# Three norms between layers: rows scaled by r on VectorE and transposed in pairs of k tiles between the first products

## The chip, the core and the metric

The kernel runs on one core of a Trainium2 chip. The metric is the device time of one execution in microseconds (us). The median of three runs of the kernel before is 2278.21 us (2277.64 to 2278.24). The engines are PE (TensorE, products and transposes), DVE (VectorE), ACT (ScalarE), POOL (GpSimd) and SP (which issues the DMAs).

## The reference, cut to what matters

Two layers work on 256 latent rows of 2048 columns. Each layer has two norms; the first norm of the first layer belongs to the start and isn't touched. The other three are all of this form (`g`, `scale` and `shift` are vectors over the 2048 columns), and each is followed by a product with a large weight:

```python
def rms_norm(x, g):
    xf = x.astype(jnp.float32)
    y = xf * lax.rsqrt(jnp.mean(xf * xf, axis=-1, keepdims=True) + EPS)
    return (y * g.astype(jnp.float32)).astype(x.dtype)

def modulate(h, shift, scale):
    return h * (1.0 + scale[:, None, :]) + shift[:, None, :]
...
    x = x + gt1[:, None, :] * yl
    x = x + gt2[:, None, :] * sq_relu_mlp(modulate(rms_norm(x, g_norm_ffn[layer]), sh2, sc2),
                                          w_ffn_up[layer], w_ffn_down[layer])
```

## The kernel before, in words

The rows lie in two blocks of 128 (`x0`, `x1`, in rows of `order` below `x_5691` and `x_5692`), the 2048 columns in 16 k tiles of 128. For a product the activations must stand transposed, as eight tiles `xt_92` to `xt_99` with a pair of k tiles each; every tile holds a rounded part and the rest of it (`split`: the rounding is an ACT CAST, L388, the rest a DVE subtraction, L389). Weights arrive in `raw` buffers of 128 x 2048 (1 MB) and are split in the same way into parts of 128 x 1024, `hi` on ACT (L184) and `lo` on DVE (L185), with three buffers for each. A part holds four k tiles of `group_b` (L255, the FFN's first product: 4 products for a k tile, two of 512 and two of 256 columns) or two of `group_a` (6 products of 512 columns for a k tile).

A norm starts in `residual`: after the last 256 columns of x are there, ACT sums their squares, DVE forms `ms`, POOL raises it to -1/2 (`rr`, L290), once for each block of rows. DVE then writes a diagonal matrix with r on it (`diag`, L434). `norm_modulate` (L349) multiplies each 128 x 128 piece of x with it, which transposes and scales in one product (`ps_t`, 32 products, which PE runs as 64 passes); then ACT or DVE applies scale and shift (`mtmp`, L381 and L379; `acol` is the column of factors, L352), and `split` writes the pair.

The three places are called norm 1 (before the first FFN, at 684 us), norm 2 (before the pool layer, at 1416 us) and norm 3 (before the second FFN, at 1545 us).

A scheduler puts the instructions of each engine into one fixed order when the program is built, by priorities: the splitting of weights has the highest (`SOONER`), the norm comes next (`FIRST`), and the background work, 320 steps `acc` on DVE (L311) that form the modulation vectors of later stages from `araw` buffers (NA4 = 7 of them), a low one (`LATER`). `hold` is a list of instructions behind which the next weight parts are put, `norm` the one behind which the background steps are put. On the chip every engine takes its instructions in that order.

Of the kernel before, what the change touches and what calls it, by code (L numbers as in the profile page):

```python
# [36 lines left out]
NA4 = 7  # L37
# [113 lines left out]
class Builder:  # L151
    def __init__(self, nc, tc, I, out):
        self.nc, self.tc, self.I, self.out = nc, tc, I, out
        self.bg = deque()
# [4 lines left out]
        self.hold, self.norm = [], None
        self.hp = None  # L160
        self.gate_pool = None
        self.nraw2 = 2
# [62 lines left out]
    def group_a(self, chunks, lhs, blocks=(0, 1), cols=512):  # L225
# [9 lines left out]
        for i, ch in enumerate(chunks):  # L235
# [4 lines left out]
            for k, b in pairs:  # L240
# [3 lines left out]
                self.mm(o, xh, h, kt + k == 0, False)  # L244
# [104 lines left out]
    def norm_modulate(self, xs, stat, sh, sc, gi):  # L349
        nc = self.nc  # L350
        a = self.tp.tile([P, KT], F32, tag="acol", bufs=1, name="acol")
        nc.vector.scalar_tensor_tensor(a, sc, 1.0, self.gcol[:, gi, :], ALU.add, ALU.mult)  # L352
# [16 lines left out]
        for kp in range(KT // 2):  # L369
            if kp >= N_PRE:  # L370
                transposed(kp, 0)
            transposed(kp, 1)
            ps = pss[kp]
# [16 lines left out]

    def keep_warm(self, n):

        ps = self.pa.tile([P, 192], F32, tag="ax", name="ps_warm")
        with self.tc.issue_after(self.last_mm):
            for _ in range(n):
                self.mm(ps, self.ident, self.mask, True, True)
# [4 lines left out]
    def residual(self, ps, c, w, gate, stat, after=None):  # L401
# [8 lines left out]
        with self.tc.high_priority(offset=FIRST):  # L410
# [9 lines left out]
            else:  # L420
# [4 lines left out]
                if after is None:  # L425
                    self.diag = self.cp.tile([P, 2, P], F32, tag="diag", bufs=1, name="diag")
                for b in range(2):
# [5 lines left out]
                    if after is None:  # L433
                        self.last_diag = nc.vector.tensor_scalar(self.diag[:, b], self.ident, self.r[b], None, ALU.mult).ins  # L434
# [514 lines left out]
    def pool_layer(self, stat, sh, sc, gate):  # L949
# [177 lines left out]
```

## Time and profile before

| | us |
|---|---|
| median of three runs | 2278.21 |
| the profiled execution, its time | 2277.29 |
| its span | 2275.5 |
| PE busy | 2240.6 (98%) |
| DVE busy | 1686.8 (74%) |
| ACT busy | 1101.2 (48%) |

The span is that of the instructions; 1.8 us of the execution's time lie around it. PE is busy nearly throughout, so time is gained or lost where PE waits or does other work than products. At the three norms PE has no products for some 10 us.

### The profile page before, as it was taken

The numbers are of one execution on the slowest core, as the hardware profiler recorded it, in microseconds if no ns is written. First come the engines' busy times: TensorE is split into PE (matmuls) and PEld (weight loads), VectorE is DVE, ScalarE is ACT, GpSimd is POOL, SyncE is SP. The second block draws the span as 40 slices with busy tenths as digits, with TensorE's granted clock in tenths as the row PEclk, the third lists the DMA queues.
The fourth block names the chain that finished last, engine by engine and source line by source line (L and its number), as shares of the span: only waits on it lengthen the run. The fifth ranks groups of instructions, "written<-read, shape, count | busy, mean of one in ns | idle before, by whom it ended". The sixth has DMA issues, their size and how long they took to land.

```text
span 2275.5 us, 31625 instructions
## 1 busy us (share of the span) xinstructions
PE 2240.6 (98%) x12514; PEld 1864.4 (82%) x12514; DVE 1686.8 (74%) x2053; ACT 1101.2 (48%) x1482; POOL 36.6 (2%) x47
## 2 busy tenths in 40 slices
PE   8999999999999999999999999999999999999998
PEld 4667788778888888888888888888888888888887
DVE  4569999988868877887888875769864655556655
ACT  4226465554446544544544554445444443443443
POOL 0000000001000000000000000000000000000000
PEclk9999999999999999999999999999999999999999
DMA  9876776777886888888888885646865555555553
GB/s 359 294 273 225 269 258 252 259 284 287 319 299 253 320 311 305 297 320 303 324 316 310 298 302 199 222 171 252 309 230 195 185 187 195 182 192 188 185 190 125
DMA packets 110637, 582.72 MB, mean 256 GB/s; under 512 B 12292, under 2 KB 12420, under 8 KB 66584
## 3 DMA queue, kind: packets, MB, share of 16 engines
q1 hardware_dynamic: 110488, 580.70, 70.3%
q8 instruction: 98, 1.61, 0.3%
q14 instruction: 51, 0.42, 0.0%
HBM read 578.55 MB, written 2.10 MB: 255 GB/s over the span
## 4 chain that ended last, share of the span: by engine, by line
PE 88%; DVE 5%; ACT 2%; issue 2%; DMA 2%; POOL 0%; SPq 0%; POOLq 0%; DVEq 0%; ACTq 0%
PE mma L221 39%; PE mmb L221 34%; PE mmf L221 4%; PE mmn L221 3%; PE mmi L221 2%; DVE acc L311 1%; DVE lo L185 1%; PE ps_as L221 1%; PE ps_o L221 1%; ACT hi L184 1%; PE ps_ada L221 1%; DVE kk L731 1%; DVE qg L731 0%; DMA raw<-in_w_fbs 0%; DMA xraw<-in_ctx 0%
## 5 line engine op out<-in xcount | busy, mean ns | idle before, releaser
L184 ACT CAST hi<-raw 128x1024 fp32r<-128x1024 f32 (+1 forms) x701 | 733.1, 1047 | 945.4 <-PE mma L221 455.1
L185 DVE TENSOR_TENSOR lo<-raw,hi 128x1024 fp32r<-128x1024 f32 (+1 forms) x701 | 849.9, 1215 | 417.3 <-ACT hi L184 416.0
L221 PE MATMUL mma<-hi,xt 128*128 128x512 f32 x2800 | 872.8, 391 | 0.5 <-DVE q L280 0.5
L221 PE MATMUL mmb<-xt,hi 128*128 128x512 f32 x2304 | 813.6, 398 | 1.1 <-DVE xt L389 0.8
L221 PE MATMUL mmb<-xt,lo 128*128 128x256 f32 x2304 | 648.1, 281 | 0.8 <-DVE lo L185 0.8
L221 PEld LDWEIGHTS mma<-hi,xt 128*128 128x128 f32 x2800 | 524.7, 188 | 111.6 <-DVE q L280 1.0
L221 PE MATMUL mma<-lo,xt 128*128 128x512 f32 x1400 | 546.4, 390 | 0.0
L221 PEld LDWEIGHTS mmb<-xt,hi 128*128 128x128 f32 x2304 | 432.9, 188 | 104.1 <-DVE xt L389 1.0
L311 DVE SCALAR_TENSOR_TENSOR acc<-araw,csil,acc 128x1024 f32<-128x1024 f32 x320 | 409.5, 1280 | 49.9 <-DMA araw<-in_wada 48.2
L221 PEld LDWEIGHTS mmb<-xt,lo 128*128 128x128 f32 x2304 | 436.2, 189 | 3.1 <-DVE lo L185 1.1
L221 PEld LDWEIGHTS mma<-lo,xt 128*128 128x128 f32 x1400 | 263.0, 188 | 55.3 <-issue 0.2
L221 PE MATMUL mmf<-xt,hi 128*128 128x512 f32 x512 | 165.1, 395 | 0.0
L221 PEld LDWEIGHTS mmf<-xt,hi 128*128 128x128 f32 x512 | 96.0, 188 | 26.6 <-ACT hi L184 4.2
L221 PE MATMUL mmf<-xt,lo 128*128 128x512 f32 x256 | 100.2, 391 | 0.0
L221 PE MATMUL mmn<-hi,xt 128*128 128x256 f32 x416 | 76.0, 283 | 0.0
L221 PEld LDWEIGHTS mmn<-hi,xt 128*128 128x128 f32 x416 | 65.3, 192 | 0.4
L221 PE MATMUL mmn<-lo,xt 128*128 128x256 f32 x208 | 58.9, 283 | 0.0
L221 PEld LDWEIGHTS mmf<-xt,lo 128*128 128x128 f32 x256 | 48.1, 188 | 9.5
L221 PE MATMUL mmi<-hi,xt 128*128 128x512 f32 x128 | 45.0, 410 | 6.2 <-ACT xt L550 4.0
L713 ACT COPY both<-kk 128x256 f32<-128x256 f32 x64 | 26.3, 411 | 50.4 <-DVE kk L731 41.6
L389 DVE TENSOR_TENSOR xt<-hup,xt 128x512 fp32r<-128x512 f32 x64 | 43.9, 687 | 8.7 <-ACT xt L388 8.5
L586 DVE TENSOR_TENSOR fbacc<-mmf,fbacc 128x1024 f32<-128x1024 f32 x24 | 29.3, 1221 | 22.1 <-PE mmf L221 22.1
(185 smaller groups left out, 1340.0 us busy)
## 6 DMA issues: line engine op xcount, KB each, us to landing
araw<-in_wada SPq DMA_DIRECT2D x320, 512.0 KB
raw<-in_w_up SPq DMA_DIRECT2D x128, 1024.0 KB
raw<-in_w_down SPq DMA_DIRECT2D x128, 1024.0 KB
sraw<-in_wada_s SPq DMA_DIRECT2D x56, 512.0 KB
raw<-in_w_out SPq DMA_DIRECT2D x16, 1024.0 KB
raw<-in_w_pool SPq DMA_DIRECT2D x16, 1024.0 KB
raw<-in_w_fb SPq DMA_DIRECT2D x10, 1024.0 KB
raw<-in_w_q SPq DMA_DIRECT2D x8, 1024.0 KB
```

The lines of the kernel that those rows point to most:

```text
L184: nc.scalar.copy(hi, raw[:, o:o + w])
L185: nc.vector.tensor_sub(lo, raw[:, o:o + w], hi.bitcast(F32))
L221: self.first_mm = self.nc.tensor.matmul(out, lhsT, rhs, start=start, stop=stop, **kw).ins
L311: nc.vector.scalar_tensor_tensor(acc, raw, self.csil[:, c, 0:1], acc, ALU.mult, ALU.add)
L389: return self.nc.vector.tensor_sub(x[:, :, lo], src, x[:, :, hi].bitcast(F32))
L586: nc.vector.tensor_add(fbacc[h], ps, fbacc[h])
L713: nc.scalar.copy(o.rearrange("p (s j i) -> p j s i", j=2, i=hh), bass.AP(src.tensor, src.offset, [list(src.ap[0]), [st + hh, 2], [seg, ns] ...
L731: nc.vector.tensor_mul(x, x, m.broadcast_to([P, ns, hh]))
```

## The change

Rows of x are scaled by r on DVE (`xn`, 128 x 256, for one pair of k tiles and one block of rows) and transposed by PE's transpose, instead of being multiplied with a diagonal matrix. `diag` goes. Three pairs are prepared at once, as before (N_PRE). The other five stand in `later` and are put out one by one between the products of the first group, ahead of each even k tile (`next_pair`). The first pair has its scale and shift, its rounding and its rest done for each k tile apart. `hold` now lets the first two weight parts go where they will and puts the third behind the first pair, the fourth behind the third pair; background steps are put behind the third pair. `hi` and `lo` get four buffers each, the background's staging six instead of seven. In the pool layer the first product is written ahead of the work on `srow` and `brow`.

```diff
-NA4 = 7
+NA4 = 6
-HELD = 1
+NW = 4
...
-            hi = self.wp.tile([P, 1024], F32R, tag="hi", bufs=3, name="hi")[:, 0:w]
-            lo = self.wp.tile([P, 1024], F32R, tag="lo", bufs=3, name="lo")[:, 0:w]
+            hi = self.wp.tile([P, 1024], F32R, tag="hi", bufs=NW, name="hi")[:, 0:w]
+            lo = self.wp.tile([P, 1024], F32R, tag="lo", bufs=NW, name="lo")[:, 0:w]
             with ExitStack() as st:
-                if self.hold:
-                    st.enter_context(self.tc.issue_after(self.hold.pop(0)))
+                behind = self.hold.popleft() if self.hold else None
+                if behind:
+                    st.enter_context(self.tc.issue_after(behind()))
...
-                        self.mm(ps[:, n], h3[:, j, n * P:n * P + P], xt[kt][:, 0:2, :], kt == 0, False)
-                        self.mm(ps[:, n, 1], l3[:, j, n * P:n * P + P], xt[kt][:, 1, :], False, kt == n_kt - 1)
+                        with self.next_pair(kt if n == 0 else 1):
+                            self.mm(ps[:, n], h3[:, j, n * P:n * P + P], xt[kt][:, 0:2, :], kt == 0, False)
+                        self.last_mm = self.mm(ps[:, n, 1], l3[:, j, n * P:n * P + P], xt[kt][:, 1, :], False, kt == n_kt - 1)
...
-        diag = self.diag
-        self.hold, self.norm = [self.last_diag], self.last_diag
-        pss = {}
+        xn, pss, done = {}, {}, {}
 
         def transposed(kp, b):
-
             if kp not in pss:
-                pss[kp] = self.pa.tile([P, 2, T], F32, tag="ax", name="ps_t")
+                xn[kp] = self.t2("xn")
+                pss[kp] = [self.pa.tile([P, 1, T], F32, tag="ax", name="ps_t") for _ in range(2)] if kp == 0 else \
+                    [self.pa.tile([P, 2, T], F32, tag="ax", name="ps_t")]
+            nc.vector.tensor_scalar(xn[kp][:, b], xs[b][:, 2 * kp * P:2 * kp * P + T], self.r[b], None, ALU.mult)
             for j in range(2):
-                kt = 2 * kp + j
-                self.mm(pss[kp][:, j, b * P:b * P + P], xs[b][:, kt * P:kt * P + P], diag[:, b], True, True)
...
+                o = pss[kp][j][:, 0] if kp == 0 else pss[kp][0][:, j]
+                self.last_mm = nc.tensor.transpose(o[:, b * P:b * P + P], xn[kp][:, b, j * P:j * P + P], self.ident).ins
+
+        def modulated(kp):
             tmp = self.t2("mtmp")
+            x = self.xt2[kp]
...
+                if j if kp == 0 else kp % 2:
+                    nc.vector.tensor_scalar(tmp[:, j], src, s, t, ALU.mult, ALU.add)
                 else:
-                    nc.scalar.activation(tmp[:, j], ps[:, j], AF.Identity, bias=t, scale=s)
-            self.hold.append(self.split(kp, 1, 0, tmp).ins)
-        self.hold = self.hold[:HELD]
+                    nc.scalar.activation(tmp[:, j], src, AF.Identity, bias=t, scale=s)
+                if kp == 0:
+                    nc.scalar.copy(x[:, j, 1], tmp[:, j])
+                    done[kp] = nc.vector.tensor_sub(x[:, j, 0], tmp[:, j], x[:, j, 1].bitcast(F32)).ins
+            if kp:
+                done[kp] = self.split(kp, 1, 0, tmp).ins
+
+        def ahead(kp):
+            with self.tc.high_priority(offset=FIRST):
+                for b in range(2):
+                    transposed(kp, b)
+                modulated(kp)
...
+        for kp in range(N_PRE):
+            transposed(kp, 1)
+            modulated(kp)
+        self.norm = done[N_PRE - 1]
+        self.later = deque(lambda kp=kp: ahead(kp) for kp in range(N_PRE, KT // 2))
+
+        self.hold = deque([None, None, lambda: done[0], lambda: done[2]])
+
+    def next_pair(self, kt):
+
+        if self.later and kt % 2 == 0:
+            with self.tc.issue_after(self.last_mm):
+                self.later.popleft()()
+            return self.tc.issue_after(self.last_mm)
+        return nullcontext()
...
-                    if after is None:
-                        self.last_diag = nc.vector.tensor_scalar(self.diag[:, b], self.ident, self.r[b], None, ALU.mult).ins
...
         self.plan(LEFT_P, 18)
+        pooled(0)
...
-        for n in range(4):
+        for n in range(1, 4):
             pooled(n)
```

How this moves instructions, at the places that the prediction speaks of. PE at norm 1 before: after the last product of the layer (not shown) the filling product `ps_warm`, all 32 products with the diagonal matrix, then the products `mmb` of the first pair:

```order
L221 MATMUL ps_warm<-small,ident 128x192
L221 MATMUL ps_t<-diag,x_5691 128x128 x8
L221 MATMUL ps_t<-diag,x_5692 128x128 x8
L221 MATMUL ps_t<-diag,x_5691 128x128 x2
L221 MATMUL ps_t<-diag,x_5692 128x128 x2
```

PE at norm 1 now, first the start and then the passage from the first pair's eight products to the second pair's:

```order
L222 MATMUL ps_warm<-small,ident 128x192
L370 MATMUL ps_t<-ident,xn 128x128 x16
L222 MATMUL mmb<-xt_92,hi 128x512
L222 MATMUL mmb<-xt_92,lo 128x256
L222 MATMUL mmb<-xt_92,hi 128x512
```
```order
L222 MATMUL mmb<-xt_92,hi 128x512
L222 MATMUL mmb<-xt_92,lo 128x256
L370 MATMUL ps_t<-ident,xn 128x128 x4
L222 MATMUL mmb<-xt_93,hi 128x512
L222 MATMUL mmb<-xt_93,lo 128x256
```

Four pairs are transposed ahead of the first product instead of eight, the others four transposes at a time between the products.

DVE at norm 1 before, from `acol` on:

```order
L352 SCALAR_TENSOR_TENSOR acol<-sc_0_101,small 128x16
L434 TENSOR_SCALAR diag<-ident,rr 128x128
L311 SCALAR_TENSOR_TENSOR acc<-araw,csil,acc 128x1024
L379 TENSOR_SCALAR mtmp<-ps_t,acol,sh_0_100 128x256 x3
L389 TENSOR_TENSOR xt_92<-mtmp,xt_92 128x2x256
L389 TENSOR_TENSOR xt_93<-mtmp,xt_93 128x2x256
L379 TENSOR_SCALAR mtmp<-ps_t,acol,sh_0_100 128x256 x2
L389 TENSOR_TENSOR xt_94<-mtmp,xt_94 128x2x256
L379 TENSOR_SCALAR mtmp<-ps_t,acol,sh_0_100 128x256
L185 TENSOR_TENSOR lo<-raw_6583,hi 128x1024 x2
L185 TENSOR_TENSOR lo<-raw,hi 128x1024
L389 TENSOR_TENSOR xt_95<-mtmp,xt_95 128x2x256
```

DVE at norm 1 now, from `acol` on, in two pieces that follow each other:

```order
L358 SCALAR_TENSOR_TENSOR acol<-sc_0_101,small 128x16
L367 TENSOR_SCALAR xn<-x_5691,rr 128x256 x3
L367 TENSOR_SCALAR xn<-x_5692,rr 128x256 x3
L380 TENSOR_SCALAR mtmp<-ps_t,acol,sh_0_100 128x256 x2
L367 TENSOR_SCALAR xn<-x_5691,rr 128x256
L367 TENSOR_SCALAR xn<-x_5692,rr 128x256
L385 TENSOR_TENSOR xt_92<-mtmp,xt_92 128x256 x2
```
```order
L380 TENSOR_SCALAR mtmp<-ps_t,acol,sh_0_100 128x256 x2
L367 TENSOR_SCALAR xn<-x_5691,rr 128x256
L367 TENSOR_SCALAR xn<-x_5692,rr 128x256
L380 TENSOR_SCALAR mtmp<-ps_t,acol,sh_0_100 128x256
L425 TENSOR_TENSOR xt_94<-mtmp,xt_94 128x2x256
L186 TENSOR_TENSOR lo<-raw_6542,hi 128x1024 x2
L186 TENSOR_TENSOR lo<-raw,hi 128x1024 x2
L425 TENSOR_TENSOR xt_95<-mtmp,xt_95 128x2x256
L367 TENSOR_SCALAR xn<-x_5691,rr 128x256
L425 TENSOR_TENSOR xt_96<-mtmp,xt_96 128x2x256
L367 TENSOR_SCALAR xn<-x_5692,rr 128x256
L425 TENSOR_TENSOR xt_93<-mtmp,xt_93 128x2x256
```

The subtraction that finishes the second pair, `xt_93`, stood second among the pairs and ahead of the weight parts; now it stands fifth, behind four `lo`. Behind it (not shown) come three `acc`, an `mtmp` and the next `lo`.

DVE at norm 3 before, from the second `diag` on, and now, from the first `lo` on (ahead of it stand the same seven rows as at norm 1):

```order
L434 TENSOR_SCALAR diag<-ident,rr 128x128
L185 TENSOR_TENSOR lo<-raw,hi 128x1024 x2
L185 TENSOR_TENSOR lo<-raw_13746,hi 128x1024
L389 TENSOR_TENSOR xt_92<-mtmp,xt_92 128x2x256
L379 TENSOR_SCALAR mtmp<-ps_t,acol,sh_1_104 128x256 x4
L389 TENSOR_TENSOR xt_94<-mtmp,xt_94 128x2x256
L389 TENSOR_TENSOR xt_93<-mtmp,xt_93 128x2x256
```
```order
L186 TENSOR_TENSOR lo<-raw_13805,hi 128x1024
L380 TENSOR_SCALAR mtmp<-ps_t,acol,sh_1_104 128x256 x2
L367 TENSOR_SCALAR xn<-x_5691,rr 128x256
L367 TENSOR_SCALAR xn<-x_5692,rr 128x256
L380 TENSOR_SCALAR mtmp<-ps_t,acol,sh_1_104 128x256
L425 TENSOR_TENSOR xt_95<-mtmp,xt_95 128x2x256
L367 TENSOR_SCALAR xn<-x_5691,rr 128x256
L367 TENSOR_SCALAR xn<-x_5692,rr 128x256
L425 TENSOR_TENSOR xt_94<-mtmp,xt_94 128x2x256
L186 TENSOR_TENSOR lo<-raw_13805,hi 128x1024
L425 TENSOR_TENSOR xt_96<-mtmp,xt_96 128x2x256
L425 TENSOR_TENSOR xt_93<-mtmp,xt_93 128x2x256
```

Three `lo` stood in DVE's row ahead of every pair; now two stand among the pairs, and `xt_93` is again the fifth pair to be finished. At norm 2 the order is like that of norm 3, with three `lo` and four pairs, `xt_93` the fourth of them.

## Rows read from the trace of the kernel before

**Rows 1.** Page, part 1: busy us, share of the span, instructions of each engine.
```profile
PE 2240.6 (98%) x12514; PEld 1864.4 (82%) x12514; DVE 1686.8 (74%) x2053; ACT 1101.2 (48%) x1482; POOL 36.6 (2%) x47
```
**Rows 2.** PE's longest entry of waits, 190 to 540 us: us, times, longest.
```profile
PE ps_sc L221 <- ACT both L713: 4.8, 7, 2.0
```
**Rows 3.** Timeline at norm 1: start us, us, engine, line, operation, count, idle before.
```profile
684.42 0.28 PE L221 MATMUL mmn<-hi,xt 128*128 128x256 f32 x1
...
687.03 0.17 DVE L352 SCALAR_TENSOR_TENSOR acol<-sc,small 128x16 f32<-128x16 f32 x1 [0.67 <-POOL rr L290]
...
687.46 5.87 PE L221 MATMUL ps_t<-diag,x 128*128 128x128 f32 x48 [0.65 <-DVE diag L434]
...
692.53 2.96 ACT L184 CAST hi<-raw 128x1024 fp32r<-128x1024 f32 x3
...
693.62 3.50 DVE L185 TENSOR_TENSOR lo<-raw,hi 128x1024 fp32r<-128x1024 f32 x3
...
694.90 0.39 PE L221 MATMUL mmb<-xt,lo 128*128 128x256 f32 x1 [0.76 <-DVE lo L185]
```
**Rows 4.** Chain in order of time, behind norms 1 and 2: start us, us, what.
```profile
694.90 88.80 PE mmb L221 x511
...
1428.25 22.93 PE mma L221 x101
```
**Rows 5.** Timeline at norm 2.
```profile
1418.76 0.18 DVE L352 SCALAR_TENSOR_TENSOR acol<-sc,small 128x16 f32<-128x16 f32 x1 [0.66 <-POOL rr L290]
...
1428.01 0.71 PE L221 MATMUL mma<-hi,xt 128*128 128x512 f32 x2
```
**Rows 6.** Timeline at norm 3.
```profile
1548.11 0.17 DVE L352 SCALAR_TENSOR_TENSOR acol<-sc,small 128x16 f32<-128x16 f32 x1 [0.66 <-POOL rr L290]
...
1552.40 1.89 DVE L379 TENSOR_SCALAR mtmp<-ps_t,acol,sh 128x256 f32<-128x256 f32 x4
...
1556.16 0.36 PE L221 MATMUL mmb<-xt,lo 128*128 128x256 f32 x1
```
**Rows 7.** DVE's groups by shape: busy us, mean ns of one, idle before.
```profile
L185 DVE TENSOR_TENSOR lo<-raw,hi 128x1024 fp32r<-128x1024 f32 x690 | 842.2, 1222 | 407.3 <-ACT hi L184 406.0
L311 DVE SCALAR_TENSOR_TENSOR acc<-araw,csil,acc 128x1024 f32<-128x1024 f32 x320 | 409.5, 1280 | 49.9 <-DMA araw<-in_wada 48.2
L389 DVE TENSOR_TENSOR xt<-mtmp,xt 128x512 fp32r<-128x512 f32 x24 | 15.8, 686 | 0.5 <-ACT xt L388 0.5
L379 DVE TENSOR_SCALAR mtmp<-ps_t,acol,sh 128x256 f32<-128x256 f32 x24 | 12.0, 537 | 0.1
L414 DVE TENSOR_TENSOR x<-x,rtmp 128x256 f32<-128x256 f32 x16 | 6.7, 422 | 0.3
L484 DVE TENSOR_SCALAR xraw<-xraw,r 128x1024 f32<-128x1024 f32 x4 | 2.9, 749 | 1.3 <-POOL r L290 1.3
L434 DVE TENSOR_SCALAR diag<-ident,rr 128x128 f32<-128x128 f32 x6 | 1.7, 283 | 1.8 <-POOL rr L290 1.8
```
**Rows 8.** Tile `ps_t` (ns min/median/max), then PE's timeline at the start.
```profile
L542 PE MATMUL ps_t<-ident,xraw x64: 272/273/455, 24.0 to 167.4; 128*128 128x128 f32 x64
...
147.01 1.07 PE L542 MATMUL ps_t<-ident,xraw 128*128 128x128 f32 x8
147.84 0.48 PE L221 MATMUL mmf<-xt,hi 128*128 128x512 f32 x1
```
**Rows 9.** Stretches: length, busy us (count) of PE, PEld, DVE, ACT, POOL; PEclk; DMA share, GB/s.
```profile
15.60:19.80 4.20, 1.66 (x18) 0.50 (x16) 1.93 (x7) 1.15 (x1) 1.20 (x2) 0.98 0.99 389
...
20.00:22.00 2.00, 1.69 (x16) 0.59 (x16) 0.39 (x1) 0.69 (x2) 0.00 (x0) 0.50 1.05 420
...
52.00:56.00 4.00, 1.11 (x5) 0.44 (x4) 3.80 (x7) 3.56 (x6) 0.00 (x0) 1.00 1.02 381
```
**Rows 10.** Chain in order of time, at the start.
```profile
26.99 2.93 PE mmi L221 x6
30.92 1.58 PE mmi L221 x6
```

More of the change, by code (lines that the diff above doesn't have):

```diff
@@ L158, in __init__ @@
         self.n_sraw = 0
-        self.hold, self.norm = [], None
+        self.hold, self.later, self.norm = deque(), deque(), None
         self.hp = None
@@ L243, in group_a @@
                 o = outs[blocks.index(b)]
-                self.mm(o, xh, h, kt + k == 0, False)
+                with self.next_pair(kt + k if b == blocks[0] else 1):
+                    self.mm(o, xh, h, kt + k == 0, False)
                 self.mm(o, xh, l, False, False)
@@ L351, in norm_modulate @@
         a = self.tp.tile([P, KT], F32, tag="acol", bufs=1, name="acol")
-        nc.vector.scalar_tensor_tensor(a, sc, 1.0, self.gcol[:, gi, :], ALU.add, ALU.mult)
+        with self.tc.high_priority(offset=SOONER):
+            nc.vector.scalar_tensor_tensor(a, sc, 1.0, self.gcol[:, gi, :], ALU.add, ALU.mult)
         self.keep_warm(N_WARM)
-        diag = self.diag
-        self.hold, self.norm = [self.last_diag], self.last_diag
-        pss = {}
+        xn, pss, done = {}, {}, {}
         def transposed(kp, b):
             if kp not in pss:
-                pss[kp] = self.pa.tile([P, 2, T], F32, tag="ax", name="ps_t")
+                xn[kp] = self.t2("xn")
+                pss[kp] = [self.pa.tile([P, 1, T], F32, tag="ax", name="ps_t") for _ in range(2)] if kp == 0 else \
+                    [self.pa.tile([P, 2, T], F32, tag="ax", name="ps_t")]
+            nc.vector.tensor_scalar(xn[kp][:, b], xs[b][:, 2 * kp * P:2 * kp * P + T], self.r[b], None, ALU.mult)
             for j in range(2):
-                kt = 2 * kp + j
-                self.mm(pss[kp][:, j, b * P:b * P + P], xs[b][:, kt * P:kt * P + P], diag[:, b], True, True)
-        for kp in range(N_PRE):
-            transposed(kp, 0)
[L369 to L373, printed above, removed]
+                o = pss[kp][j][:, 0] if kp == 0 else pss[kp][0][:, j]
+                self.last_mm = nc.tensor.transpose(o[:, b * P:b * P + P], xn[kp][:, b, j * P:j * P + P], self.ident).ins
+        def modulated(kp):
             tmp = self.t2("mtmp")
+            x = self.xt2[kp]
             for j in range(2):
@@ L377, in norm_modulate, with keep_warm @@
                 s, t = a[:, kt:kt + 1], sh[:, kt:kt + 1]
-                if kp % 2:
-                    nc.vector.tensor_scalar(tmp[:, j], ps[:, j], s, t, ALU.mult, ALU.add)
-                else:
-                    nc.scalar.activation(tmp[:, j], ps[:, j], AF.Identity, bias=t, scale=s)
-            self.hold.append(self.split(kp, 1, 0, tmp).ins)
-        self.hold = self.hold[:HELD]
+                src = pss[kp][j][:, 0] if kp == 0 else pss[kp][0][:, j]
+                if j if kp == 0 else kp % 2:
+                    nc.vector.tensor_scalar(tmp[:, j], src, s, t, ALU.mult, ALU.add)
+                else:
+                    nc.scalar.activation(tmp[:, j], src, AF.Identity, bias=t, scale=s)
[10 more added lines that the diff above has]
+        for kp in range(N_PRE):
+            transposed(kp, 0)
+        for kp in range(N_PRE):
+            transposed(kp, 1)
[9 more added lines that the diff above has]
+        return nullcontext()
+    def keep_warm(self, n):
+        ps = self.pa.tile([P, 192], F32, tag="ax", name="ps_warm")
+        with self.tc.issue_after(self.last_mm):
+            for _ in range(n):
+                self.last_mm = self.mm(ps, self.ident, self.mask, True, True)
     def split(self, kp, hi, lo, src):
@@ L389, in split @@
         return self.nc.vector.tensor_sub(x[:, :, lo], src, x[:, :, hi].bitcast(F32))
[L391 to L396, printed above, removed]
     def grow(self, gate, c, w):
@@ L424, in residual @@
                 self.r = [self.cp.tile([P, 1], F32, tag="rr", bufs=4, name="rr") for _ in range(2)]
-                if after is None:
-                    self.diag = self.cp.tile([P, 2, P], F32, tag="diag", bufs=1, name="diag")
                 for b in range(2):
@@ L432, in residual @@
                     self.rstd(ms, self.r[b], 1)
-                    if after is None:
-                        self.last_diag = nc.vector.tensor_scalar(self.diag[:, b], self.ident, self.r[b], None, ALU.mult).ins
         for b in range(2):
```

## The prediction

> **What bounds the kernel now.** The page's first part comes first [rows 1]: PE is busy for 2240.6 us, 98% of the span. So a change counts by what it does to the stretches in which PE has no products, and three of those lie at the norms. The timeline there shows their length. At norm 1 the last product of the layer starts at 684.42, and the stream of products begins at 694.90; between them lie the products with `diag` and the waits [rows 3]. What ends the wait is DVE: `acol` starts at 687.03, once POOL has the second r, and the first `lo` is done 7.87 us after that. At norm 2 the distance from `acol` to the stream is 1428.01 - 1418.76 = 9.25 us with 5 products done before it [rows 5], at norm 3 1556.16 - 1548.11 = 8.05 us, also with 5 done [rows 6]. I count everything from `acol`, since the way to it (last product, residual, squares, POOL) is untouched. In the stream one FFN product takes 88.80 / 511 = 0.174 us, one of the pool layer 22.93 / 101 = 0.227 us [rows 4].
>
> **The change, part by part.** *PE's own work.* 64 passes with `diag` for each norm go and 32 transposes come. Eight transposes stand within 0.83 us (147.01 to 147.84), 0.104 us each [rows 8]; I take 0.107. The passes cost at most 5.87 / 48 = 0.122 us [rows 3]. That is 32 x 0.107 = 3.4 us instead of up to 7.8 for each norm. It would be the gain if PE were what is waited for. It isn't: at all three norms the stream begins when DVE lets it, so this saving counts only where it lies behind that point.
>
> If transposes didn't overlap, each would take its whole duration of 0.273 us [rows 8]; 32 of them would be 8.7 us, and the 12 that stand behind the critical point below would add 12 x (0.273 - 0.107) = 2.0 us at each norm, 6 in all. The Trainium skill ("TensorE: Matmul & The Clock Gate", Part 4: PE-mode transpose) gives about 275 ns for a transpose in a kernel's context and would so lead a reader to that sum. The trace agrees with it as a duration; as a distance it shows 0.104.
>
> *DVE's work.* `diag` goes (0.28 us, twice), 16 `xn` come. The trace has no such shape. The line through 128 columns (283 ns) and 1024 columns (749 ns) gives 350 ns at 256; its bounds are 283 and the 422 of an addition of 256 columns [rows 7]. Back to back, instructions overlap: three `lo` of 1.222 take 3.50, so 1.14 apart [rows 3], four `mtmp` of 0.537 take 1.89, so 0.45 apart [rows 6], an overlap of 0.085. That gives 0.265 for an `xn`, 0.34 for half of a pair's subtraction (422 ns), 0.60 for a whole one (686 ns).
>
> *The order on DVE is the term that decides.* DVE takes its row in order, and the changed row puts the second pair's subtraction, `xt_93`, behind others. PE's row puts the second pair's products straight behind the first pair's eight and four transposes; they wait for `xt_93`. What stands ahead of it from `acol` on, norm 1: `acol` 0.09, 12 `xn` 3.18, 5 `mtmp` 2.25, two halves of `xt_92` 0.68, `xt_94`, `xt_95`, `xt_96` 1.80, four `lo` 4.56, then `xt_93` itself 0.69. Sum 13.25, with PE's wake-up 13.3 us. None of these waits for long on others by my count: ACT's first `hi` can start some 4.6 us after `acol` (before it: one `mtmp`, three casts, two `mtmp`) and then runs 0.95 apart [rows 3], ahead of the `lo`. So pair 2 begins 13.3 us after `acol`, where before the whole stream began at 7.87. By then 8 of 128 products of the first two outputs are done. PE can't use the gap: its row is in order too.
>
> Behind `xt_93` stand three `acc` of 1.28 (each on the sum of the one before, 1.32 apart), an `mtmp` and the next `lo`: 3.96 + 0.45 + 1.22 = 5.6 us, so that `lo` is there at 18.9. PE reaches the product that needs it after 17 products and 4 transposes, 13.3 + 3.4 = 16.7: another wait of 2.1. Norm 1 to the end of the second output: 13.3 + 120 x 0.174 + 12 x 0.107 + 2.1 = 37.6 us; before, 7.87 + 127 x 0.174 = 30.0. **Norm 1: +7.6.**
>
> Norm 3 has two `lo` ahead of `xt_93` instead of four: 13.25 - 2.28 = 10.97, so 11.0; then the same, 11.0 + 20.9 + 1.3 + 2.2 = 35.4. Before: 8.05 + 123 x 0.174 = 29.45. **Norm 3: +5.9.**
>
> Norm 2: 11 `xn` 2.92, 5 `mtmp` 2.25, halves 0.68, two pairs 1.20, three `lo` 3.42, `acol` 0.09, `xt_93` 0.69: 11.25, so 11.3. PE has 14 of the first output's 96 products done by then (the second pair's first two need no subtraction): 11.3 + 82 x 0.227 + 12 x 0.107 = 31.2, and some 0.5 for a pair's `xn` behind a `lo`: 31.7. Before: 9.25 + 91 x 0.227 = 29.9. **Norm 2: +1.8.**
>
> *The clock.* Until now each hole was filled with products with `diag`; now PE has 16 short transposes and eight products in some 15 us. In this trace PE's granted clock fell to 0.50 (1.2 GHz) at 20 us, after a stretch of 4.2 us with 1.66 us of work [15.6 to 19.8, rows 9]; it stayed at 1.00 through 52 to 56 us with 1.11 us of work in 4 [rows 9]. Six products at the low clock took 2.93 us instead of 1.58 [rows 10], and the clock was back behind them: 1.35 us for a fall. I take one fall in the three norms, +1.4; bounds 0 and three falls with their transposes, about +5.
>
> *The buffers.* Fourth `hi` and `lo`: no gain in the stream, where PE waits for no part [rows 4], 511 products without a stop. In the mixer PE's largest wait is for `both`, 4.8 us [rows 2], behind a full DVE; an earlier `lo` may take some of it, a missing staging buffer may add to DVE's 48.2 us of waits for `araw` [rows 7]. I take 0, from -4.8 to +2.4 (two of those 1.2 us waits on the path). *`pooled(0)` moved ahead*: the work on `srow` and `brow` goes behind the first product, where PE has products for 20 us; 0, and if that cover is gone 1 to 2 us once.
>
> **Sum.** 7.6 + 1.8 + 5.9 + 1.4 = 16.7 on the execution's own 2277.29: 2294.0. The median of the runs lies 0.92 above that execution, so 2295 us.
>
> **Rivals.** *DVE keeps up, PE is the bound (not slower).* Place: the second pair at norms 2 and 3. If `xt_93` were there when the first pair's products end, the stream would begin 3.9 us after `acol` (`acol`, eight `xn`, two `mtmp`, the halves: 0.09 + 2.12 + 0.90 + 0.76) with 16 transposes still to pay, 1.7: 5.6 against 8.05 - 5 x 0.17 = 7.2 at norm 3 and 9.25 - 1.1 = 8.1 at norm 2; nothing at norm 1, where the weights themselves are late (first `hi` at 692.53 [rows 3]). Gain 1.6 + 2.5 = 4.1, with the median 2274. It decides from the point where `xt_93` ends under 5.6 us after `acol`; some 5.5 us of work would have to leave DVE's row. With the wait of 4.8 us in the mixer gone too [rows 2] it would be 2269. For it: PE's work does shrink. Against it: the row above.
>
> *The buffers pay part back.* The wait of 4.8 us goes and the clock holds: 2295 - 4.8 - 1.4 = 2289; if part of the wait at norm 1 is filled as well, some 2284.
>
> *The clock falls at every norm and the transposes run at half pace:* 2295 + 2 x 1.4 + 1 to 3 = 2299 to 2301. *The transposes don't overlap:* 2295 + 6 = 2301; the rows speak against it, 0.02. (That is the Trainium skill's 275 ns taken as a distance.)
>
> That the change doesn't do what it says, transposes between products, is no case: the order shows that it does, for four of the eight pairs.
>
> **How the numbers follow.** My forecast (the order on DVE decides, 2290 to 2299) 0.70; clock (0.08) or transposes (0.02) dearer, 2299 to 2302: 0.10; buffers pay back (2284 to 2290) 0.08; the holes half of what I sum and the buffers' gain on top (2278 + 8 - 5 = 2281) 0.06; DVE keeps up 0.06, of which 0.02 at 2274 and 0.04 with the buffers' gain at 2269. A difference under 0.2% (4.6 us) can't be told from none here. Slower by over 0.2%: 0.70 + 0.10 + 0.08 = 0.88; within: 0.06 + 0.02 = 0.08; faster 0.04. The range, 2285 to 2302, leaves out the last two cases and the edge of the third.
>
> **What would show it.** Right: PE's waits of the changed kernel list `mmb` for the DVE subtraction of the second pair at 4 us, twice, and for `lo` at 2 us; the distance from `acol` to the first product on `xt_93` is 13.3, 11.3 and 11.0 us; the stretches between the norms are as long as before. `xn` at 0.35 us and transposes 0.107 us apart show the terms; the granted clock in the holes shows the fall. Wrong: if the second pair's products follow the first pair's without a wait, the order isn't what sets them; if the holes are as summed and the time isn't, the buffers in the mixer moved it.

## The result, and the profile after

The changed kernel takes 2296.6 us (median of 5 runs, 2295.07 to 2299.78) against 2278.24 for the kernel before, measured beside it. The ratio is 1.0079, interval 1.0067 to 1.0091: it is slower by 18 us. The forecast was 2295.

PE's work has hardly changed, and its waits have. Page, part 1, of the changed kernel (engine, busy us, share, instructions), to be held against [rows 1]:

```profile
PE 2240.1 (98%) x12418; PEld 1859.1 (81%) x12418; DVE 1698.0 (74%) x2101; ACT 1102.8 (48%) x1482; POOL 35.7 (2%) x47
```

PE's longest waits in the whole changed kernel (engine, tile and line waited with, what for: us, times, longest); [rows 2] was the longest before:

```profile
PE mmb L222 <- DVE xt L425: 7.6, 2, 4.2
PE ps_t L370 <- DVE xn L367: 6.4, 6, 2.7
...
PE ps_s L222 <- ACT kwt L764: 2.9, 4, 1.3
...
PE mma L222 <- ACT xt L424: 2.1, 1, 2.1
PE ps_sc L222 <- ACT both L738: 2.0, 4, 0.9
...
PE mma L222 <- DVE xt L425: 1.1, 1, 1.1
```

The products now wait for activations. Where that is, the timeline at norm 1 shows (start us, us, engine, line, operation, count, idle before). It answers to [rows 3]:

```profile
688.28 3.89 ACT L185 CAST hi<-raw 128x1024 fp32r<-128x1024 f32 x4
...
690.47 4.63 DVE L186 TENSOR_TENSOR lo<-raw,hi 128x1024 fp32r<-128x1024 f32 x4
691.74 0.29 PEld L222 LDWEIGHTS mmb<-xt,lo 128*128 128x128 f32 x1 [2.08 <-DVE lo L186]
...
692.07 1.14 ACT L424 CAST xt<-mtmp 128x512 fp32r<-128x512 f32 x2
...
695.01 0.69 DVE L425 TENSOR_TENSOR xt<-mtmp,xt 128x512 fp32r<-128x512 f32 x1
...
696.84 0.69 DVE L425 TENSOR_TENSOR xt<-mtmp,xt 128x512 fp32r<-128x512 f32 x1 [0.88 <-ACT xt L424]
697.45 0.35 DVE L367 TENSOR_SCALAR xn<-x,rr 128x256 f32<-128x256 f32 x1
697.71 0.69 DVE L425 TENSOR_TENSOR xt<-mtmp,xt 128x512 fp32r<-128x512 f32 x1
698.31 3.92 DVE L314 SCALAR_TENSOR_TENSOR acc<-araw,csil,acc 128x1024 f32<-128x1024 f32 x3
...
698.55 0.53 PE L222 MATMUL mmb<-xt,hi 128*128 128x512 f32 x1 [3.45 <-DVE xt L425]
```

`acol` starts at 683.59 here. PE has the first pair's products behind it at 694, transposes the next pair, and then waits 3.45 us. DVE is never free in that time but for 0.88 us: it splits four weight parts and finishes three other pairs, and the subtraction at 697.71 is that of the second pair. At norm 3 the same wait is 4.15 us, at norm 2 2.13 and 1.15.

One measure serves for all runs below: how far behind `acol` ACT starts to copy out the second output of the FFN (`half`, norms 1 and 3), or the first of the pool layer (`ph`, norm 2). It is ACT's time: the copy starts 0.9 to 1.5 us behind the end of PE's last product, as ACT has other work in hand or not (0.03 at norm 2 of e12). In the kernel before these copies are, in ACT's timeline:

```profile
718.01 0.57 ACT L279 COPY half<-mmb 128x512 f32<-128x512 f32 x1
...
1450.12 1.00 ACT L965 CAST ph<-mma 128x1024 fp32r<-128x1024 f32 x1
...
1578.60 0.58 ACT L279 COPY half<-mmb 128x512 f32<-128x512 f32 x1
```

and in the changed kernel, where `acol` starts at 683.59, 1424.86 and 1558.95:

```profile
723.88 0.57 ACT L282 COPY half<-mmb 128x512 f32<-128x512 f32 x1
...
1461.10 1.01 ACT L990 CAST ph<-mma 128x1024 fp32r<-128x1024 f32 x1
...
1596.71 0.58 ACT L282 COPY half<-mmb 128x512 f32<-128x512 f32 x1
```

With the `acol` of [rows 3, 5, 6], the distances were 30.98, 31.36 and 30.49 us and are 40.29, 36.24 and 37.76: 21.5 us longer in all. The stretches between the norms are as they were (700.98 against 700.75 us, 97.85 against 97.99, and 696.99 against 696.90 to the end). The start, up to the first `acol`, is 3.44 us shorter in this execution. 21.46 - 3.44 + 0.23 - 0.14 + 0.09 = 18.20, which is the difference of the two spans, 2293.7 - 2275.5.

### The profile page after: what moved, and what is told of

It is laid out like the page before. It is cut to its first block, busy times and chain, and to the rows that moved or that the text cites. A ratio compares the mean times of both kernels' runs of the same rounds, so it can differ in the third digit from the quotient of the medians.

```text
span 2293.7 us, 31514 instructions
## 1 busy us (share of the span) xinstructions
PE 2240.1 (98%) x12418; PEld 1859.1 (81%) x12418; DVE 1698.0 (74%) x2101; ACT 1102.8 (48%) x1482; POOL 35.7 (2%) x47
## 4 chain that ended last, share of the span: by engine, by line
PE 84%; DVE 9%; DMA 3%; ACT 2%; issue 2%; POOL 0%; SPq 0%; POOLq 0%; DVEq 0%; ACTq 0%
PE mma L222 38%; PE mmb L222 34%; PE mmf L222 4%; DVE acc L314 3%; DVE lo L186 2%; PE mmi L222 2%; PE mmn L222 2%; PE ps_as L222 1%; DMA araw<-in_wada 1%; DVE qg L756 1%; ACT hi L185 1%; DVE kk L756 1%; PE ps_ada L222 1%; PE ps_t L370 0%; DMA raw<-in_w_fbs 0%
## 5 line engine op out<-in xcount | busy, mean ns | idle before, releaser
L283 DVE TENSOR_TENSOR hup<-mmb,half 128x512 f32<-128x512 f32 x64 | 43.8, 684 | 0.0
```

Source lines behind the costliest of these rows:

```text
L283: self.nc.vector.tensor_add(out, ps[:, :, 1], half)
```

## The experiments

All numbers in one table: medians of the runs, and from one profiled execution each the start of `acol` at norm 1 and the three distances.

| kernel | us | `acol` at | norm 1 | norm 2 | norm 3 | sum |
|---|---|---|---|---|---|---|
| before | 2278.2 | 687.0 | 30.98 | 31.36 | 30.49 | 92.8 |
| changed | 2296.6 | 683.6 | 40.29 | 36.24 | 37.76 | 114.3 |
| e1 three buffers | 2300.4 | 683.9 | 41.86 | 34.21 | 37.15 | 113.2 |
| e2 second pair first | 2291.3 | 688.6 | 35.52 | 32.42 | 34.66 | 102.6 |
| e3 all pairs ahead | 2292.5 | 684.0 | 38.30 | 32.71 | 34.28 | 105.3 |
| e4 more filling | 2297.2 | 687.1 | 40.14 | 35.76 | 36.69 | 112.6 |
| e5 no later xn | 2294.1 | 689.4 | 36.59 | 31.74 | 37.28 | 105.6 |
| e6 = e2 + e3 | 2285.8 | 693.7 | 36.89 | 29.11 | 32.33 | 98.3 |
| e9 = e6 + filling | 2284.6 | 683.9 | 34.12 | 31.61 | 32.12 | 97.9 |
| e10 = e6 + ACT | 2284.4 | 683.5 | 36.40 | 28.78 | 33.67 | 98.9 |
| e11 = e9 + e10 | 2286.3 | 687.2 | 33.52 | 31.61 | 32.23 | 97.4 |
| e12 norm 2 alone | 2282.9 | 691.6 | 30.98 | 29.49 | 30.53 | 91.0 |

In e7 and e8 `acol` itself was moved; their distances are taken from the end of POOL's second r, 0.03 us ahead of `acol` elsewhere: e7 2290.0 us, 38.85, 28.82, 30.32; e8 2295.0 us, 40.40, 30.42, 31.68.

The changed kernel, e2 to e6 and e9 to e11 have the same instructions in the same order on PE, DVE, ACT and SP up to norm 1 (but for filling products at its door), and yet reach `acol` between 683.5 and 693.7. That is the scatter of the stretch before it, 10 us, and why the distances say more here than a median.

The distances have two limits. They are those of one execution each, and they leave out what is paid back behind the norm. The stretches between the norms and to the end, against the kernel before, are together longer by 3.7 us in e1, 5.6 in e3, 1.7 in e5, 2.1 in e6, 2.9 in e9 and 0.6 in e2: in e3 PE waits 1.5 us for the sum of the first output (`hup`) right behind norm 1, and in e6 1.2 us behind norm 2 for `pl`, the rest of the pool layer's first output. By the medians, e2 takes back 5.3 us and e6 10.8 of the 18.4 that the changed kernel lost; from `acol` on, their profiled executions are 11.3 and 14.1 us shorter than the changed one's.

**e1, the buffers.** Three part buffers and seven staging buffers again:

```diff
-NA4 = 6
+NA4 = 7
...
-NW = 4
+NW = 3
```

> The changed kernel with three hi and lo buffers and seven staging buffers again; all else stays. The order theory (xt_93 stands too far back in DVE's row): the waits for xt_93 at the norms stay at 2 to 4 us each; at norm 1 only three lo stand ahead of xt_93, so the distance from acol to its first product falls from 14.95 us by one lo (1.14). Of the 3.4 us by which the changed kernel reaches acol of norm 1 earlier (683.6 against 687.0): if the buffers bring them, acol is back at 687 and the time is 2297 to 2300; if they are scatter of the stretch before, acol stays between 683 and 685 and the time is 2294 to 2297. A rival, that the smaller staging costs time at the norms, would give under 2290.

2300.35 us, ratio to before 1.0100 (1.0081 to 1.0119). `acol` is at 683.93, so an early start comes without the new buffers too. The second pair's products at norm 1 begin 12.53 us behind `acol`, 2.4 sooner than with four, where 1.14 was expected: PE's waits for `xt_93` shrink to 0.8 us there and 2.3 at norm 3. But the waits of its transposes for `xn` grow from 6.4 to 12.3 us in all (3.0 at once at norm 1), so that norm 1 as a whole is 1.6 longer and the three distances add up to only 1.1 less. The median lies 3.8 above that of the changed kernel; the stretches behind norms 1 and 2 are 1.2 and 2.4 us longer than there. The intervals of the two overlap. Four buffers are no cause of the loss; whether they save those us in general stays open.

**e2, the second pair first.** One priority is altered:

```diff
         for kp in range(N_PRE):
             transposed(kp, 1)
-            modulated(kp)
+            with self.tc.high_priority(offset=2 * SOONER if kp in (1,) else 0):
+                modulated(kp)
```

> The changed kernel with one thing altered: scale, shift, rounding and rest of the second pair get a higher priority than the weight parts, so that xt_93 is finished right behind xt_92 and ahead of every lo. The order theory: the waits of PE for xt_93 (3.45 and 4.15 us, and 2.13 + 1.15 at norm 2, 10.9 in all) go; some of it comes back as later waits, since the weight parts and the other pairs stand further back; 2287 to 2291 us, and the second half copy comes 2 to 4 us nearer to acol at each norm (now 40.3, 36.2 and 37.8). The rival that DVE's whole work in the norm is the limit (16 xn more, in whatever order): another wait of the same size takes its place, 2294 to 2297. The rival that the transposes between the products cost PE the time: no change either, 2294 to 2297, but without new waits.

2291.27 us (ratio 1.0057, 1.0040 to 1.0074), distances shorter by 4.8, 3.8 and 3.1, 11.7 in all. The wait for `xt_93` is gone at all three norms. PE's waits at norm 1, first the changed kernel, then e2:

```profile
PE mmb L222 <- DVE xt L425: 3.4, 1, 3.4
PE ps_t L370 <- DVE xn L367: 3.3, 2, 2.7
PE mmb L222 <- DVE lo L186: 1.6, 1, 1.6
```
```profile
PE ps_t L370 <- DVE xn L367: 4.2, 3, 2.7
PE mmb L222 <- ACT hi L185: 1.3, 1, 1.3
PE mmb L222 <- DVE lo L186: 1.0, 2, 0.8
```

The instructions are the same; only their order differs. The order theory holds for half of the distance lost. Part of that half is the clock: without the hole at norm 2 it does not fall there. The norm 2 stretch of the changed kernel and that of e2 (columns of [rows 9]):

```profile
1424.86:1461.10 36.24, 31.80 (x134) 25.45 (x135) 24.27 (x44) 16.48 (x25) 0.00 (x0) 0.86 0.43 152
```
```profile
1425.36:1457.78 32.42, 27.56 (x134) 22.11 (x135) 24.54 (x44) 16.39 (x25) 0.00 (x0) 1.00 0.48 170
```

At norm 2 part of the wait came back in another place: the waits of transposes for `xn` grew from 1.4 to 5.1 us, 2.9 of them at later pairs, whose `xn` now stand behind `lo`.

**e3, all pairs ahead.** The loop of the kernel before (all eight pairs in `norm_modulate`), with all else of the change:

```diff
-        for kp in range(N_PRE):
+        for kp in range(KT // 2):
+            if kp >= N_PRE:
+                transposed(kp, 0)
             transposed(kp, 1)
             modulated(kp)
...
-        self.later = deque(lambda kp=kp: ahead(kp) for kp in range(N_PRE, KT // 2))
+        self.later = deque(lambda kp=kp: ahead(kp) for kp in ())
```

> The changed kernel with all eight pairs prepared in norm_modulate, as before, instead of five of them between the products; xn, transposes, hold and buffers stay. xt_93 then stands ahead of the lo. The order theory: the waits for xt_93 go, 2286 to 2291, and what is left above 2278 is the work of the xn on DVE (16 x 0.27 = 4.3 us for each norm, not all of it on the path). The rival that the xn cost it and not the place of the pairs: 2293 to 2297. The rival that this half of the change is free and only the placing between products costs: 2275 to 2279.

2292.49 us, between the first and second expectation. The distances are 9.0 us shorter than in the changed kernel, but most of that is paid back: the stretch behind norm 1 is 2.8 us longer than there, with the wait for `hup` in it, and the one to the end 2.3. At norm 1 `xt_93` now stands ahead of every `lo`, and the wait for it is gone; the 1.5 us for an `xt` that are left there come late, at the first product on the eighth pair, `xt_99`. At norms 2 and 3 `xt_93` still stands behind three and two `lo`, and PE waits 2.3 and 1.3 us for it.

**e4, more filling.** `N_WARM = 6` in the changed kernel.

> The changed kernel with six filling products instead of one ahead of the wait for r at each norm (5 x 0.5 = 2.5 us of PE's wait for POOL, which is 3.4 us at norm 3, 2.3 to 2.7 at norm 1 and 0.9 at norm 2); DVE's row at norm 1 is the same. Clock as the main cause: the granted clock stays at 1.00 through the first transposes and the products of the first pair, and the time falls by 4 us or more, under 2293. The order theory: the first transposes run at the high clock, but the waits for xt_93 stay at 3 to 4 us and the clock falls in them; at most 1.5 us are gained at norms 1 and 3 and about 1.5 lost at norm 2, so 2294 to 2298.

2297.22 us. The waits for `xt_93` stayed at 3.4 and 4.2 us, and the distances fell by 0.15, 0.48 and 1.07. The clock held through the first transposes and fell in the hole behind them, as the order theory had it. The second pair's products began 14.46, 12.30 and 11.20 us behind `acol`, for 14.95, 11.83 and 12.04 in the changed kernel; at norms 1 and 3 the rows of DVE and ACT are the same in both. At norm 2, where I expected a loss, there was none. Stretches of e4 at norm 1 (PE, PEld, DVE, ACT, POOL busy with counts; then the granted clock; DMA share, GB/s):

```profile
687.00:690.00 3.00, 1.55 (x12) 1.26 (x12) 2.89 (x10) 1.16 (x3) 0.02 (x1) 1.00 0.69 208
690.00:692.00 2.00, 0.63 (x4) 0.42 (x4) 2.00 (x7) 1.85 (x5) 0.00 (x0) 1.00 0.99 418
692.00:694.00 2.00, 0.79 (x1) 0.28 (x1) 2.00 (x5) 2.00 (x3) 0.00 (x0) 0.68 0.76 320
694.00:696.00 2.00, 1.28 (x4) 1.18 (x5) 2.00 (x3) 2.00 (x3) 0.00 (x0) 0.50 0.00 0
```

**e5, fewer xn.** Five pairs are transposed without having been scaled, so this kernel leaves out r for them:

```diff
-            nc.vector.tensor_scalar(xn[kp][:, b], xs[b][:, 2 * kp * P:2 * kp * P + T], self.r[b], None, ALU.mult)
+            src = xs[b][:, 2 * kp * P:2 * kp * P + T]
+            if kp < N_PRE:
+                nc.vector.tensor_scalar(xn[kp][:, b], src, self.r[b], None, ALU.mult)
+                src = xn[kp][:, b]
...
```

> The changed kernel without the xn of the five later pairs: their transposes take x itself, so the scaling by r is left out for them (10 of 16 xn fewer at each norm, 10 x 0.27 = 2.7 us of DVE's work). In DVE's row at norm 1 xt_93 still stands behind four lo. The order theory: PE still waits for xt_93 at norms 1 and 3, each wait shorter by the four xn that stood ahead of it (1.1 us), 2.3 and 3.1 us; second half copy 1 to 2 us nearer to acol at each norm (now 40.3, 36.2, 37.8); 2291 to 2294 us. The rival that DVE's work as such is the limit: each norm 2.7 us or more shorter, 2287 to 2290. The rival that the place of the transposes between the products costs PE the time: nothing changes, 2295 to 2298.

2294.12 us, 0.1 above the range of the order theory, but the distances fell by 3.7, 4.5 and 0.5, 8.7 in all, where 2.7 each was DVE's work and 1 to 2 each the order's. Of the waits for `xt_93`, 0.65 us is left at norm 1 and 3.56 at norm 3, where 2.3 and 3.1 were expected; at norm 2 the granted clock stayed at 1.00, as in e2. The order on DVE changed with the `xn` gone, so this run doesn't part the two theories.

**e6, both repairs.** e3 with the priority of e2.

> Both repairs of the order in one: all eight pairs prepared ahead, and the second pair's work ahead of the weight parts. The order theory: with no wait for xt_93 left and the pairs in the order of their use, below either of the two repairs alone (2291.3 and 2292.5): 2283 to 2288, second half copies at 35, 31.5 and 33 us from acol. The rival that the xn's work on DVE is what is left in both: no lower than 2290, since the same 16 xn are done. The rival that the order alone is what the changed kernel loses by: 2276 to 2280.

2285.77 us (10 runs; 1.0028, 1.0017 to 1.0039), as expected. Of the 21.5 us 16.0 are gone from the distances, with all 48 `xn`, all 96 transposes and the buffers in place. Norm 2 is now 2.3 us shorter than before the change, of which 1.3 are paid back in the stretch behind it. Norms 1 and 3 are longer by 5.9 and 1.8, and of norm 1 the stretches show why:

```profile
695.60:697.60 2.00, 1.54 (x8) 1.14 (x6) 1.27 (x3) 1.40 (x4) 0.00 (x0) 0.50 1.02 434
...
701.60:703.60 2.00, 1.73 (x6) 1.53 (x7) 2.00 (x3) 1.61 (x2) 0.00 (x0) 0.50 0.00 0
703.60:705.60 2.00, 2.00 (x8) 1.71 (x8) 2.00 (x4) 0.00 (x0) 0.00 (x0) 0.50 0.74 225
705.60:709.00 3.40, 3.40 (x16) 2.83 (x14) 1.50 (x3) 1.57 (x2) 0.00 (x0) 0.67 1.01 426
```

From 703.6 on PE has all it needs and runs at the low clock.

**e9, filling that holds the clock.** e6 with filling products in the holes:

```diff
-N_WARM = 1
+N_WARM = 6
...
             transposed(kp, 1)
+            self.keep_warm({2: 4, 3: 4}.get(kp, 0))
```

> The kernel with both repairs of the order (2285.8) with filling products in PE's holes at each norm: five more ahead of the wait for r, four behind the first twelve transposes and four behind the next four; DVE's row at norm 1 is the same. What is left there: from 2 us after r to 14 us after it PE's granted clock is 0.50, and some 16 products stand 0.32 us apart instead of 0.174. If the clock is what is left: it stays near 1.00, norm 1 falls from 36.9 to about 34 us and norm 3 from 32.4 to 31; norm 2, which has no such hole, may lose up to 1; 2280 to 2284 us. If DVE is what is left, the products wait for DVE instead of running slowly: distances within 0.7 of the run before, 2284 to 2288.

2284.55 us. Norm 1 fell from 36.89 to 34.12, as forecast for the clock, and the granted clock is 1.00 throughout:

```profile
692.00:694.00 2.00, 2.00 (x14) 1.73 (x13) 2.00 (x3) 0.73 (x1) 0.00 (x0) 1.00 0.38 70
694.00:696.00 2.00, 2.00 (x13) 1.57 (x11) 2.00 (x4) 1.56 (x2) 0.00 (x0) 1.00 0.86 365
```

The rows of DVE and ACT are those of e6 there. At norms 2 and 3 they changed a little as well: norm 3 fell by 0.2 only, and norm 2 rose by 2.5; it had no hole to be filled, and the filling now stands in PE's way. The sum fell by 0.5, the median by 1.2, inside the scatter and within the range of the other expectation. So the clock was 2.8 us of norm 1, and filling of one size for all three norms loses most of it again at norm 2.

**e10 and e11, less on DVE.** e6 and e9 with scale and shift of pairs 4, 6 and 8 on ACT:

```diff
-                if j if kp == 0 else kp % 2:
+                if j if kp == 0 else kp == 1:
```

> The kernel with both repairs of the order (2285.8) with scale and shift of pairs 4, 6 and 8 on ACT instead of DVE: 6 x 0.45 = 2.7 us of DVE's work less at each norm, 6 x 0.47 = 2.8 of ACT's more. If DVE's work is what is left: each norm 1 to 2.5 us shorter, 2279 to 2283. If the clock and the late weights of norm 1 are: within 0.7 at norm 1, 2284 to 2288.

> Both of the runs before in one: filling products and scale and shift on ACT. If each takes a part of what is left, they add: 2276 to 2281, level with the kernel before. If only one of them is a cause, no better than the better of the two.

2284.38 and 2286.28 us; neither comes level with the kernel before. e10's distances change by -0.5, -0.3 and +1.3, e11's against e9 by -0.6, 0 and +0.1. The second pair is the cleaner one: the granted clock is 1.00 at all three norms of both, while at norm 3 its mean is 0.86 in e10 and 0.95 in e6. With 2.7 us less on DVE and 2.8 more on ACT nothing is gained, so DVE's work alone isn't what is left.

**e7, parts ahead of r.** The kernel of e10 with the first chunk of weights loaded and split ahead of `acol`:

```diff
         self.rate = 0.0
+        first = self.load_w(I[f"w_up{l}"][0])
...
-        with self.tc.high_priority(offset=SOONER):
+        with self.tc.high_priority(offset=SOONER), self.tc.issue_after(self.last_lo):
             nc.vector.scalar_tensor_tensor(a, sc, 1.0, self.gcol[:, gi, :], ALU.add, ALU.mult)
...
-        self.hold = deque([None, None, lambda: done[0], lambda: done[2]])
+        self.hold = deque([lambda: done[1], lambda: done[2]])
```

> The kernel of the run before, with two alterations: the first two weight parts are loaded and split ahead of acol (their weights lie in the buffer before r is there, while DVE and ACT wait), and pairs 4, 6 and 8 take scale and shift on ACT instead of DVE (6 x 0.45 = 2.7 us off DVE). If what stands behind the wait for r on DVE is the limit, two lo (2.3 us) and 2.7 us leave it at each norm: second half copies at 31, 29.5 and 31 us from acol, 2274 to 2281, level with the kernel before. The rival that the granted clock, low after the hole at the start of each norm, is what is left: the distances stay above 33, and 2284 to 2288. A danger: acol itself is put behind the two lo, and if the weights come late it starts later.

(The expectation speaks of the run before; e10, without the moved parts, ran only later.) 2290.02 us. At norm 3 the two parts do fit ahead of r, and 30.32 us is the shortest distance there of all runs. At norm 1 the danger came true, in ACT's timeline:

```profile
687.70 0.42 ACT L447 ACTIVATE rtmp<-x 128x256 f32<-128x256 f32 x1 [2.37 <-DVE x L446]
688.02 0.19 ACT L447 ACTIVATION_READ_ACCUMULATOR rtmp<-x 128x1 f32 x1
693.84 3.88 ACT L185 CAST hi<-raw 128x1024 fp32r<-128x1024 f32 x4 [5.63 <-DMA raw<-in_w_up]
```

r is there at 689.04, the first weights of the FFN only at 693.84. That is 4.8 us behind r; in e8 the same wait ends 4.85 behind r, and the changed kernel's first `hi` stands at 688.28, 4.7 behind its r. Norm 1 can't begin its stream earlier, whatever DVE does. SP's rows say why: it issues that load only when POOL's second r is done, 0.02 us behind its end. First SP's wait, which the changed kernel has in the same length, then the issue:

```profile
SPq L174 <- POOL rr L293: 11.1, 1, 11.1
```
```profile
689.06 0.81 SPq L174 DMA_DIRECT2D raw<-in_w_up  x2
```

In the kernel before, too, the load is issued at 687.03, 0.03 us behind r. So these parts could not lie ready before r, as the expectation had it. What ties the load to r, and what an earlier issue would give, wasn't tried.

**e8, the same in the kernel before.**

> The kernel before (diagonal matrix, three buffers) with the first two weight parts loaded and split ahead of acol. At norm 1 the stream waited for the first lo until 7.87 us after acol, and the parts took 3.5 us of DVE behind it; with two lo ahead of acol the stream should begin 2 to 3 us nearer to acol at norm 1 and 1 to 2 at norm 3, where DVE is the one that is waited for: 2273 to 2276 us. The rival that acol is pushed back by as much: 2277 to 2280.

2294.97 us, 15.4 slower than the kernel before beside it, outside both expectations. ACT waited 5.68 us for the same weights at norm 1, with `acol` and PE's passes behind it (PE waited 9.0 us once for an `mtmp`); norm 1 took 40.40 us, the stretch behind it 4.6 more. The prediction had called the weights of norm 1 late by the first `hi` [rows 3]; this expectation gave that up, and the run bears it out.

**e12, norm 2 alone.** The kernel before with e6's form at norm 2 only (gi is the norm's index):

```diff
...
+        if gi == 2:
+            return self.norm_rows(xs, stat, sh, sc, gi)
...
```

> The kernel before with the new form (rows scaled on DVE, real transposes, all pairs prepared ahead, the second pair ahead of the weight parts) at norm 2 alone; norms 1 and 3, the three part buffers and seven staging buffers stay as before. In the repaired kernels norm 2 took 28.8 to 29.1 us from r to the first split of the pool layer, against 31.4 before, and the next stretch up to 1.3 us longer. If the form pays at that norm by itself: 2275 to 2278 (1 to 2.3 us under the kernel before, about what the measurement can just tell). If the gain at the norm is given back in the stretches behind it, or came from the buffers: 2277.5 to 2280, no difference.

2282.85 us (11 runs; 1.0017, 1.0007 to 1.0027), slower than both expectations. Norm 2 is 1.9 us shorter, norms 1 and 3 are as before to 0.04. Most of the 1.9 is the measure's: in the kernel before ACT runs a CAST ahead of the copy, in e12 it stands ready when PE's last product ends (first the kernel before, then e12):

```profile
1449.17 1.05 ACT L184 CAST hi<-raw 128x1024 fp32r<-128x1024 f32 x1 [1.87 <-DMA raw<-in_w_pool]
```
```profile
1455.05 1.02 ACT L1019 CAST ph<-mma 128x1024 fp32r<-128x1024 f32 x1 [1.66 <-PE mma L222]
```

By the end of PE's last product norm 2 is 0.7 us shorter. The stretches between are longer, 702.98 against 700.75 and 100.93 against 97.99. There PE now waits, which it did not before:

```profile
PE mma L222 <- DVE lo L186: 1.1, 1, 1.1
...
PE mma L222 <- DVE lo L186: 0.8, 1, 0.8
PE mma L222 <- ACT hi L185: 0.7, 1, 0.7
```

What is won at the norm is lost behind it. The first of these waits stands ahead of norm 2, where all engines still have the order of the kernel before; like its `acol` at 691.6, that is scatter. No version that was run beats the kernel before.

## Why the prediction was right, and where it was off

**The mechanism was right.** The second pair's subtraction behind the weight parts is what PE waits for: 3.45 and 4.15 us at norms 1 and 3, where 4 was forecast. e2, which moves that one pair, takes away the waits and 11.7 of 21.5 us of distance; e6, which also takes the pairs out of the products, 16.0. The `xn` take 347 ns (350 estimated), six of them 1.66 us.

**The distances to the second pair** were 14.95, 11.83 and 12.04 us for 13.3, 11.3 and 11.0. The sum walked DVE's row alone and held that none of it waits for long. DVE did wait, 0.88 us at norm 1, for a CAST on ACT: ACT's row has four `hi` ahead of the casts of two pairs (688.28 to 692.17), and the pair behind them was transposed only after the first pair's products, which waited for the first `lo` and ran at the low clock. In e4, where the clock holds through the first transposes, the distance is 0.5 us shorter at norm 1 and 0.8 at norm 3, so at norm 3 most of the excess is the clock's.

**The clock is the term that was mis-sized**: 1.4 us, bounds 0 and 5. It fell twice at each norm, first about the wait for r (its mean is 0.56 over 684.30 to 691.70, 0.63 over 1424.80 to 1429.00, 0.62 over 1558.90 to 1563.40) and again about the wait for the second pair, and stayed low through the first products behind that:

```profile
698.50:702.26 3.76, 3.71 (x13) 3.32 (x14) 3.69 (x4) 1.05 (x1) 0.00 (x0) 0.55 0.60 229
1436.65:1442.83 6.18, 6.14 (x16) 4.88 (x17) 1.46 (x4) 1.04 (x1) 0.00 (x0) 0.50 0.37 151
1570.95:1576.16 5.21, 5.17 (x17) 4.59 (x18) 5.04 (x5) 1.05 (x1) 0.00 (x0) 0.51 0.87 329
```

These are 9, 12 and 13 products with four transposes each. At the full clock (0.174 or 0.227 a product, 0.107 a transpose) they take 2.0, 3.15 and 2.7 us; they took 3.7, 6.15 and 5.2. That is 7.2 us. I had priced one fall by six products of the start; here 13 to 17 instructions ran at the low clock behind each wait, at all three norms. That is what the rival with a fall at every norm describes, to which I gave 0.08. The time alone doesn't part it from the forecast, as the sum below shows; the granted clock does.

**The second waits for `lo`**, 2.1 and 2.2 us at norms 1 and 3, were 0.38 and none. PE at half pace reached those products after DVE had the parts. The low clock took their place, so that norms 1 and 3 are off by 1.7 and 1.4 only (9.3 and 7.3 for 7.6 and 5.9). At norm 2, where the sum had no such wait, the clock's 3.0 came on top: 4.9 for 1.8.

**The buffers and `pooled(0)` at nothing**: e1 shows no gain of the buffers at the norms; a few us elsewhere stay open. In the mixer the wait for `both` fell from 4.8 us [rows 2] to 2.0, as the prediction held possible, but one of 2.9 for another ACT tile, `kwt`, came in its place. The stretch from norm 2 to norm 3, with `pooled(0)`'s rows in it, is 97.85 us for 97.99: nothing, as taken.

**The sum** was 16.7 us on a profiled execution, and the three norms cost 21.5. In the execution that was profiled the start gave 3.4 of it back, by a scatter that nine kernels with one order show; with the start of the kernel before it would have taken 2299, the upper edge of the forecast and the lower one of that rival. The time came within 2 us of 2295 partly by that luck.

**The transposes** overlap as forecast: at norm 3 four of them take 0.63 us, and the shortest single one 0.27, so they stand 0.12 apart. The rival in which they don't is out. (The Trainium skill, "TensorE: Matmul & The Clock Gate", Part 4: PE-mode transpose, gives about 275 ns for one; these runs show that as the duration at the high clock, and not as the distance.)

**What is left in e6** at norm 1 against the kernel before is 5.9 us. The clock is 2.8 of it (e9). 16 of the 32 transposes stand in the stream, 1.7 by 0.107 each; before, all 64 passes lay ahead of it, in a wait that the late weights make anyway [rows 3], and the granted clock was 1.00 there. The last 0.6 is ACT's copy, which starts 1.46 us behind the end of PE's last product instead of 0.87, because the sum of the first output (`hup`) comes late from DVE. That makes 5.1; only the clock's part was tested.

## What to carry to other kernels

Where engines run in fixed orders, walk the row of the engine that feeds the next needed operand, and the row of each engine that feeds that one. A product moved into a stream pulls its whole chain of small operations behind the weight parts. Work that only fills a wait, like the passes with the diagonal matrix, can be free and still keep the clock up: taking it out gains nothing and costs the clock. Before a repair starts something earlier, look when its data land and what their load waits for. And look behind the place that a repair mends: part of a gain there can be paid back in the next stretch.

## What the runs showed of the hardware

The granted clock fell to 0.50 (1.2 GHz) at each of the three norms, about waits of PE of 2.1 to 4.2 us, and its mean was still 0.50 to 0.55 through the next 3.7 to 6.2 us, in which PE had products and transposes without a pause. In e9, with those holes filled, it stayed at 1.00 at norm 1. Four transposes in a row took 0.60 to 0.63 us at the high clock and 1.05 to 1.08 at the low one.

The same instruction order reached norm 1 at 683.5 to 693.7 us, while the distances behind it repeat to some tenths (norm 2 in e9 and e11, which differ only in where scale and shift run: 31.61 and 31.61). One profile can't tell a gain of 3 us in the stretch before norm 1 from none.
